# Branch units and merge of a hybrid streaming encoder: where loads and stores are issued, and how deep they are buffered

## The chip, the cores and the metric

The kernel runs on 1 core of one Trainium2 chip. The metric is device time in microseconds (us) of one execution, as the median of several runs.

## The reference, cut to what matters

One step of a one-layer encoder: 1024 frames of a new stream (the prompt) and 64 frames of a running one (the sample), 1088 frames in all, with 1024 channels. The part around the change is the mixer:

```python
def mixer(xn, conv_prefix, attn_fn, w_in, w_conv, w_conv_out, w_attn_out, w_out):
    proj = xn @ w_in
    cb, cc, ch, q, k, v, ga, gb = jnp.split(proj, splits, axis=-1)
    cv, conv_state = causal_conv(cc * ch, conv_prefix, w_conv)
    ya = (cb * cv) @ w_conv_out
    o, new_k, new_v = attn_fn(heads(q), heads(k), heads(v))
    yb = o.reshape(B, L, ATT_DIM) @ w_attn_out
    merged = jax.nn.sigmoid(ga) * ya + jax.nn.sigmoid(gb) * yb
    return merged @ w_out, conv_state, new_k, new_v
```

Ahead of it stands an RMSNorm, behind it the residual, a SwiGLU FFN with its own norm and residual, and a last norm. Everything is fp32. The kernel gets fp32 accuracy from fp32r matmuls by splitting each operand into a high part (a cast on ScalarE, line 128) and a low part (a subtraction on VectorE, line 129): three matmuls, high x high, high x low and low x high, make one product.

## The kernel before, in words

The frames are the moving side, in two halves of 544 columns (HT): 512 prompt frames and 32 sample frames each. A half is two pieces of 272 (HN).

**Units.** A `Unit` (line 202) is a block of a weight matrix, 256 output channels wide. `run` (line 253) multiplies it in seven steps (`STEPS`, line 134) instead of eight block products, after Strassen's manner; the sums of weight blocks are made by `Unit.prep` on DVE. A unit has `nk` row tiles per block: four in the units of `w_in`, where a step is 24 matmuls, and two in the four ya units, where it is 12. After a step ScalarE copies the bank to a staging place (`shot`, line 259), or VectorE adds a copy to the bank (`done`). Steps 1, 6, 5 and 3 write one bank, tagged A; steps 7 and 4 another, D. While a unit runs, `ahead` prepares the weights of the next one. Each unit's raw weights come by one load on SP into `rpool` (line 82), which has two buffers of 8 KB a partition under one tag, `raw`.

The list `units` (line 530) runs q, k, cc, ch, ga, cb, cc, ch, ga, cb, ga and then ya0 to ya3. The ya units multiply `w_conv_out` with the gated convolution, whose operand forms are made in the SBUF scratch `scr` during unit 12 (`uforms`, line 674). `ya_done` (line 697) multiplies a result with its gate row (`gated_load`, line 691, brings it back from `ga_d`) and stores it by SP to `y_d`; ya3 is stored without the gate, whose rows come later as `ga_rows`. Results and snapshots sit in four places of `scr` (`SNAP`, line 365), taken in turn by `slot` (line 369): a ya unit takes four.

**Plan.** The weights of the gates and of `w_attn_out` are listed in `plan` (line 300): ten entries of 128 channels for the gates gb 0 to 7 and ga 6 and 7, then eight for the attention output. Two entries share one load (a pair), also in `rpool`. `prep` (line 309) loads and splits them; `next_w` (line 325) calls it two entries ahead. `plain_load(0)` is called at the start of the last unit, n = 16, and `PlainNext` (line 803) prepares three entries during it.

**Gates and attention.** Gate rows gb are multiplied in four pieces each (`gate`, line 877) and stored by GpSimd to `gb_d`; between pieces `between` (line 1101) takes some steps of attention. `head_load` (line 902) brings the next head's rows by SP.

**Merge.** For each m of 8 output row tiles (line 1157): the attention product yb, then sigmoid(gb), times yb, plus the ya row, split into `mg` and, for the sample frames, `ms`. `rows_in` (line 1109) loads a row `yg` of `y_d` and a row `gb` of `gb_d`, each 128 x 1088, into the tiles that the queries had: `yg` in tag q1 with three buffers, `gb` in tag q0 with two. Two rows are asked for ahead of the loop, and row m + 2 at the end of step m.

**Output product.** `wo_half(0)` (line 1192) loads half of `w_out` and splits it into eight moving pairs; the loop at line 1249 multiplies nine tiles of frames in `ORDER` (line 171: 8, 0, 1, 4, 2, 5, 3, 6, 7). Tile 8 is the 64 sample frames, read from `ms`; the others are read from `mg`. The results go by GpSimd to `x1_d`, and a second loop, over the other half of `w_out`, reads them back.

The order of instructions in an engine's queue is not that of the code: the framework orders each queue by its own estimate of when things become ready, and puts in the waits. Within a queue the order is then fixed.

Of the kernel before, what the change touches and what calls it, by code (L numbers as in the profile page):

```python
# [8 lines left out]
F32 = mybir.dt.float32  # L9
# [6 lines left out]
P = 128  # L16
# [4 lines left out]
T = TP + TS  # L21
# [11 lines left out]
HT = T // 2  # L33
# [33 lines left out]
def encoder_kernel(ctx: ExitStack, tc: tile.TileContext, ins, outs):  # L67
    nc = tc.nc
# [131 lines left out]
        return temps[1][:, temps[0] % 2]  # L200

    class Unit:
        def __init__(self, src, nm, nk=4):
            self.nm, self.nk = nm, nk
            self.raw = rpool.tile([P, 2 * nk, 2 * P], F32, tag="raw", name=f"raw{nm}")
            nc.sync.dma_start(self.raw, src.rearrange("(k p) n -> p k n", p=P))
            self.w, self.s1 = {}, None

        def block(self, r, c):
            nk = self.nk  # L210
# [89 lines left out]
    plan = []  # L300

    def plain_load(i):
        ld, kt, at = plan[i]
        if "raw" not in ld:
            raw = rpool.tile([P, kt, ld["w"]], F32, tag="raw", name=f"rawp{i}")
            nc.sync.dma_start(raw, ld["src"].rearrange("(k p) n -> p k n", p=P))
            ld["raw"] = raw

    def prep(upto):
        while prep.n < min(upto, len(plan)):  # L310
            plain_load(prep.n)
            ld, kt, at = plan[prep.n]
            w = []
            for k in range(0, kt, 4):
                nm = f"p{prep.n}_{k}"
                hi, lo = pair(nm, ld.get("at", 0))
                split(hi, lo, ld["raw"][:, k : k + 4, at : at + P])
                w.append((hi, lo))
            plan[prep.n] = w
            prep.n += 1  # L320
# [43 lines left out]
    V32 = [10288]  # L364
    SNAP, STAGE, CC, UT = [544 * i for i in range(4)], [2720, 3808, 9264], [4896, 5988], [7080, 8172]
    KF = [CC[0], 2176, CC[1]]
    turn = {}

    def slot(places, n):

        k = turn[tuple(places)] = turn.get(tuple(places), -1) + 1
        a = places[k % len(places)]
        return scr[:, a : a + n]
# [157 lines left out]
    for nm, u in (  # L531
# [2 lines left out]
    ):  # L534
        base = {"q": C_Q, "k": C_K, "cc": C_CC, "ch": C_CH, "cb": C_CB, "ga": C_GA}[nm]
        units.append((nm, u, w_in[:, base + 2 * u * P : base + 2 * (u + 1) * P]))
    for u in range(4):
        units.append(("ya", u, ins["w_conv_out"][0][:, 2 * u * P : 2 * (u + 1) * P]))

    def unit_of(n):  # L540
        nm, u, src = units[n]
        return Unit(src, f"{nm}{u}", 2 if nm == "ya" else 4)

    normed(ORDER[0])
    normed(ORDER[1])
# [27 lines left out]
    late, due = [], []  # L573

    def snap1(key, nm):
        return slot(SNAP, HT)

    def whole(t, src, snap):

# [3 lines left out]
        else:  # L583
            vec.tensor_tensor(two, src, snap, op=ALU.add)

    def summed(src, snap):

        if snap is None:
            t = snap1(None, None)
            whole(t, src, None)  # L590
            return t
        vec.tensor_tensor(snap, src, snap, op=ALU.add)
        return snap.rearrange("p j n -> p (j n)")
# [55 lines left out]
    def row_of(dst, u, r, h):  # L649
        return dst[(2 * u + r) * P : (2 * u + r + 1) * P, h * HT : (h + 1) * HT]  # L650
# [40 lines left out]
    def gated_load(u):  # L691
        at = [CC[0], CC[0] + HT, CC[1], CC[1] + HT] if u % 2 == 0 else [STAGE[j] + i * HT for j in range(2) for i in range(2)]
        for a, (r, h) in zip(at, ((0, 0), (1, 1), (1, 0), (0, 1))):
            t = gated[u, r, h] = scr[:, a : a + HT]
            nc.sync.dma_start(t, row_of(ga_d, u, r, h))

    def ya_done(u):
        def f(r, h, src, snap):
            if u == 3:
                s = summed(src, snap)  # L700
            else:
                g = gated.pop((u, r, h))
                if snap is None:
                    s = snap1(None, None)
                    two = [t.rearrange("p (j n) -> p j n", j=2) for t in (s, g)]
                    vec.tensor_tensor(two[0], src, two[1], op=ALU.mult)
                else:
                    s = summed(src, snap)
                    vec.tensor_tensor(s, s, g, op=ALU.mult)
            nc.sync.dma_start(row_of(y_d, u, r, h), s)  # L710

        return f

# [109 lines left out]
    for n in range(len(units)):  # L823
        if n in (5, 6):
            for j in range(2):
                table_store(2 * (n - 5) + j)
        if n in (4, 5):
            for j in range(2):
                table_load(2 * (n - 4) + j, slot(STAGE, 768))
        if n == 0:  # L830
            r, si = r0, 2
        else:
            if n + 1 < len(units):
                nxt_unit = unit_of(n + 1)
                new = [(nxt_unit, {1: (), 2: (0, 1, 2)} if n == 1 else {})]
            else:
                new = [(PlainNext(), {})]
                plain_load(0)
            if n == 1:
                ahead += new  # L840
                r, si = r1, 2
            else:
                r, si = run1(n, unit, new), 0
            unit = nxt_unit
        if n >= 12 and n < 15:
            gated_load(n - 12)
        for _ in r:
            if n == 12:
                uforms(si)
            if n < 2 and si in (2 + n, 5 + n):  # L850
                i = 2 * n + si // 5
                cache_tile(i)
                if i + 2 < 4:
                    cache_load(i + 2)
            if si > 1:
                for f in due:
                    f()
                due.clear()
            due += late
            late.clear()  # L860
            si += 1
# [195 lines left out]
    def row_tile(l, nm):  # L1057
        return qp.tile([P, T], F32, tag=f"q{l}", name=nm, bufs=2 + l)
# [48 lines left out]
    rows = {}  # L1107

    def rows_in(m):
        t, z = rows[m] = row_tile(1, f"yg{m}"), row_tile(0, f"gb{m}")  # L1110
        nc.sync.dma_start(z, gb_d[m * P : (m + 1) * P])
        nc.sync.dma_start(t, y_d[m * P : (m + 1) * P])

# [13 lines left out]
    for i in range(4, len(GATES)):  # L1127
        gate_w[i] = next_w()
        if i == len(GATES) - LAST:
            for _ in steps:  # L1130
                pass
            att_stack.close()
            uo = pg_stack.enter_context(tc.tile_pool(name="uo", bufs=1, reuse_waits="tile"))
            uo.tile([P, 48], F32, name="pad_ob")
            t = uo.tile([P, 2, 4 * T + 8], F32R, name="ob")[:, :, : 4 * T]
            ob = Acts(t.rearrange("p l (k t) -> p l k t", k=4))
            ga_rows = [uo.tile([P, T], F32, name=f"ga{m}") for m in (6, 7)]
            for k in range(2):
                split(ob.t[:, 0, k], ob.t[:, 1, k], o_rows[k])
            late_r = row_tile(1, "rc2"), row_tile(0, "rc3")  # L1140
            for k, r in zip((2, 3), late_r):
                o = ob.t[:, 0, k].bitcast(F32)
                nc.sync.dma_start(o, o_d[k * P : (k + 1) * P])
                rc_load(r, k)
                vec.tensor_tensor(r, o, r, op=ALU.mult)
                split(ob.t[:, 0, k], ob.t[:, 1, k], r)
            rows_in(0)
            rows_in(1)
        for c in range(4):
            gate(i, (c,))  # L1150
            between()
# [4 lines left out]
    psum2 = pg_stack.enter_context(tc.tile_pool(name="psum2", bufs=2, space=PSUM, reuse_waits="tile"))  # L1156
    for m in range(8):
        wb = next_w()
        t, z = rows.pop(m)
        act.activation(z, z, AF.Sigmoid)  # L1160
        if m >= 6:
            vec.tensor_tensor(t, t, ga_rows[m - 6], op=ALU.mult)
        for h in range(2):
            yb = psum2.tile([P, 2, 512], F32, tag="mm", name=f"yb{m}_{h}")
            for j in range(2):
                product(yb[:, j, :HN], wb, ob, h * HT + j * HN, HN)
            hs = slice(h * HT, (h + 1) * HT)
            zh, th = z[:, hs], t[:, hs]
            two = zh.rearrange("p (j n) -> p j n", j=2)
            vec.tensor_tensor(two, yb[:, :, :HN], two, op=ALU.mult)  # L1170
            vec.tensor_tensor(th, th, zh, op=ALU.add)
            split(mg.at(0, m, h * HT, HT), mg.at(1, m, h * HT, HT), th)
            split(ms[:, m, 0, 32 * h : 32 * h + 32], ms[:, m, 1, 32 * h : 32 * h + 32], th[:, 512:])
        if m + 2 < 8:
            rows_in(m + 2)
    pg_stack.close()


# [62 lines left out]
    if True:  # L1241
# [4 lines left out]
        two_sums = early.tile([P, 2, D], F32, tag="raw", name="two_sums")  # L1246
        taken[0] += 1
        w = wo_half(0)
        for i in ORDER:
            t0, n = TT[i]  # L1250
            xt = wp.tile([P, D], F32, tag="xg", name=f"xr{i}")[:, :512]
            nc.sync.dma_start(xt[:n], x_rows(i)[:, :512])
            ps = bank2("BD", f"wo0_{i}")[:, 0]
            token_product(ps, i, mg_rows(i), KD, lambda k: w[k])
            residual(i, ps, xt, 512, f"o0_{i}")
            nc.gpsimd.dma_start(x1_d[t0 : t0 + n, :512], xt[:n])
# [563 lines left out]
```

## Time and profile before

| | us |
|---|---|
| median of 3 runs | 1474.4 |
| lowest, highest | 1472.62, 1477.31 |
| the profiled execution | 1474.73 |
| its span, first to last instruction | 1472.9 |
| TensorE busy in the span | 1451.7 |
| VectorE busy | 1002.8 |
| ScalarE busy | 688.0 |
| GpSimd busy | 131.8 |

The profile is of one execution. "PE Aya L274 <- ACT scr L261" reads: the TensorE instruction of line 274 that writes a tile Aya waited for the ScalarE instruction of line 261 that writes `scr`. In a row of the timeline the idle time ahead of an instruction and what ended it stand in brackets. A matmul's record is longer than its share of the pipeline: matmuls that follow each other overlap, so the time of a group is taken from start to start. Some names: `rawya` is the raw weight of a ya unit, `rawp` that of a pair of the plan, `wor` that of `w_out`. SPq is SP's queue of transfers, POOLq GpSimd's.

### The profile page before, as it was taken

The numbers are of one execution on the slowest core, as the hardware profiler recorded it, in microseconds if no ns is written. First come the engines' busy times: TensorE is split into PE (matmuls) and PEld (weight loads), VectorE is DVE, ScalarE is ACT, GpSimd is POOL, SyncE is SP. The second block draws the span as 40 slices with busy tenths as digits, with TensorE's granted clock in tenths as the row PEclk, the third lists the DMA queues.
The fourth block names the chain that finished last, engine by engine and source line by source line (L and its number), as shares of the span: only waits on it lengthen the run. The fifth ranks groups of instructions, "written<-read, shape, count | busy, mean of one in ns | idle before, by whom it ended". The sixth has DMA issues, their size and how long they took to land.

```text
span 1472.9 us, 26291 instructions
## 1 busy us (share of the span) xinstructions
PE 1451.7 (99%) x10128; PEld 1362.4 (92%) x10128; DVE 1002.8 (68%) x1845; ACT 688.0 (47%) x1368; POOL 131.8 (9%) x241
## 2 busy tenths in 40 slices
PE   9999999999999999999999999999999999999997
PEld 6899999999999998997889999999999999888886
DVE  7975565658347778583489767666666668957676
ACT  7654443435356777541356444444444445512223
POOL 1400010000011111000000111110111111000000
PEclk9999999999999999999999999999999999999999
DMA  8686521225876666664432443443344448867675
GB/s 287 183 272 224 193 66 64 66 86 167 261 211 187 183 187 193 211 201 130 149 119 80 153 164 143 168 140 119 130 158 164 151 160 304 288 233 249 213 267 205
DMA packets 161597, 262.49 MB, mean 178 GB/s; under 512 B 18528, under 2 KB 94496, under 8 KB 161472
## 3 DMA queue, kind: packets, MB, share of 16 engines
q1 hardware_dynamic: 140928, 196.13, 42.0%
q0 software_dynamic: 19392, 62.58, 11.8%
q10 hardware_dynamic: 1152, 2.10, 0.4%
q8 instruction: 80, 1.31, 0.4%
q14 instruction: 45, 0.37, 0.1%
HBM read 171.78 MB, written 90.81 MB: 178 GB/s over the span
## 4 chain that ended last, share of the span: by engine, by line
PE 88%; DVE 5%; DMA 3%; ACT 2%; issue 1%; SPq 0%; DVEq 0%; ACTq 0%
PE Ab L274 9%; PE Aa L274 8%; PE A L1733 8%; PE Db L274 4%; PE Da L274 4%; PE D L1733 4%; PE g L339 2%; PE g L340 2%; PE Aga L274 2%; PE g L338 2%; PE B L1733 2%; PE Ba L274 2%; PE Bb L274 2%; PE wo L1214 2%; PE wo L1216 2%; PE wo L1215 2%
## 5 line engine op out<-in xcount | busy, mean ns | idle before, releaser
L338 PE MATMUL g<-xn,wp 128*128 128x272 f32 x320 | 94.0, 294 | 0.0
L339 PE MATMUL g<-xn,wp 128*128 128x272 f32 x320 | 93.4, 292 | 0.0
L340 PE MATMUL g<-xn,low 128*128 128x272 f32 x320 | 93.3, 291 | 0.0
L128 ACT CAST ring<-w2r 128x512 fp32r<-128x512 f32 (+1 forms) x78 | 43.1, 588 | 97.1 <-PE A L1733 50.9
L937 DVE CUSTOM_DVE_ANT_0 p<-s,bb 128x640 f32<-128x640 f32 (+5 forms) x72 | 47.5, 661 | 39.8 <-PE s L980 37.5
L1733 PE MATMUL A<-ring,low 128*128 128x512 f32 x264 | 72.4, 389 | 0.0
L1733 PE MATMUL A<-ring,ht 128*128 128x512 f32 x264 | 72.2, 389 | 0.0
L129 DVE TENSOR_TENSOR low<-rawa,wa 128x512 fp32r<-128x512 f32 x55 | 37.8, 688 | 42.0 <-ACT wa L128 42.0
L338 PEld LDWEIGHTS g<-xn,wp 128*128 128x128 f32 x320 | 60.3, 188 | 0.9
L339 PEld LDWEIGHTS g<-xn,wp 128*128 128x128 f32 x320 | 60.2, 188 | 0.6
L340 PEld LDWEIGHTS g<-xn,low 128*128 128x128 f32 x320 | 60.3, 188 | 0.4
L1733 PEld LDWEIGHTS A<-ring,low 128*128 128x128 f32 x264 | 49.6, 188 | 10.3
L1733 PEld LDWEIGHTS A<-ring,ht 128*128 128x128 f32 x264 | 49.5, 188 | 10.3
L274 PE MATMUL Ab<-tt,wb 128*128 128x272 f32 x352 | 57.8, 286 | 0.4 <-ACT wb L128 0.4
L129 DVE TENSOR_TENSOR ring<-w2r,ring 128x512 fp32r<-128x512 f32 (+1 forms) x78 | 49.0, 648 | 13.4 <-ACT ring L128 13.4
L274 PE MATMUL Ab<-mg,wb 128*128 128x272 f32 x352 | 58.0, 286 | 0.0
L947 ACT ACTIVATE p<-p,mx 128x640 f32<-128x640 f32 (+5 forms) x72 | 50.8, 706 | 15.4 <-DVE mx L937 13.8
L274 PE MATMUL Aa<-mg,wa 128*128 128x272 f32 x352 | 57.7, 285 | 0.0
L274 PE MATMUL Aa<-tt,wa 128*128 128x272 f32 x352 | 57.7, 285 | 0.0
L128 ACT CAST wa<-rawa 128x512 fp32r<-128x512 f32 x55 | 34.0, 621 | 47.4 <-PE Ab L274 33.3
L128 ACT CAST wb<-rawb 128x512 fp32r<-128x512 f32 x55 | 34.0, 620 | 38.6 <-PE Aa L274 24.4
L1214 PE MATMUL wo<-low,mg 128*128 128x512 f32 x128 | 51.5, 402 | 0.0
(580 smaller groups left out, 4503.9 us busy)
## 6 DMA issues: line engine op xcount, KB each, us to landing
h_d<-hq POOLq DMA_DIRECT2D x44, 512.0 KB, 4.7
ht<-h_d SPq DMA_DIRECT2D x77, 256.0 KB, 3.6
low<-h_d SPq DMA_DIRECT2D x77, 256.0 KB, 3.8
h_d<-hq_early POOLq DMA_DIRECT2D x29, 512.0 KB, 4.8
rawa<-in_w_ff SPq DMA_DIRECT2D x11, 1024.0 KB, 6.5
rawb<-in_w_ff SPq DMA_DIRECT2D x11, 1024.0 KB, 5.3
w2r<-in_w_ff SPq DMA_DIRECT2D x11, 1024.0 KB, 8.1
qd<-q_d SPq DMA_DIRECT2D x32, 272.0 KB, 4.0
```

The source lines that it names most:

```text
L128: a = act.copy(hi, src)
L129: b = vec.tensor_tensor(lo, src, hi.bitcast(F32), op=ALU.subtract)
L274: newest[0] = mm(t[:, j, :HN], w[:, k, :], x[p][:, k, l, j * HN : (j + 1) * HN], start=p in (1, 2, 7) and k == 0 and n == 0, stop=k == las ...
L338: mm(out, a, first, start=k == 0, stop=False)
L339: mm(out, a, then, start=False, stop=False)
L340: mm(out, b, p, start=False, stop=k == kt - 1)
L937: vec.tensor_tensor_reduce(out=s if len(ps.shape) == 2 else s.rearrange("p (a b) -> p a b", a=2), in0=ps, in1=bias if len(ps.shape) == 2 e ...
L947: act.activation(s, s, AF.Exp, bias=mx, scale=-1.0, accum_out=sm)
L1214: mm(ps, x(k, 0), wh, start=f, stop=False)
L1215: mm(ps, x(k, 1), wh, start=False, stop=False)
L1216: mm(ps, x(k, 0), wl, start=False, stop=e)
L1733: mm(t, ht[k][:, j, x], w[:, l], start=p in (1, 2, 7) and k == 0 and n == 0, stop=k == len(ks) - 1 and n == 2, skip_group_check=p in (6, 5 ...
```

## The change

The raw weights of the four ya units come in two loads of 512 columns, both issued when unit 13 is built, at the start of unit 12, and each unit gets a view of them. Snapshots and results of the ya units take turns in ten places: the four of before, two in the third place of `STAGE`, and four in `UT`. Their stores to `y_d` are issued by GpSimd instead of SP. `prep` asks for the load two entries on whenever it comes to an entry, and `plain_load(0)` is called at unit 14 instead of unit 16. The rows `yg` get a pool of their own with five buffers, the rows `gb` take the tags q1 and q0 by turns; three rows are asked for ahead of the merge, and row m + 3 at the start of step m. The first output loop takes the tiles 0, 1, 2, 3, 8, 4, 5, 6, 7.

```diff
@@ -200,11 +200,14 @@
         return temps[1][:, temps[0] % 2]
 
     class Unit:
-        def __init__(self, src, nm, nk=4):
+        def __init__(self, src, nm, nk=4, raw=None):
             self.nm, self.nk = nm, nk
+            self.w, self.s1 = {}, None
+            if raw is not None:
+                self.raw = raw
+                return
             self.raw = rpool.tile([P, 2 * nk, 2 * P], F32, tag="raw", name=f"raw{nm}")
             nc.sync.dma_start(self.raw, src.rearrange("(k p) n -> p k n", p=P))
-            self.w, self.s1 = {}, None
 
         def block(self, r, c):
             nk = self.nk
@@ -309,6 +312,8 @@
     def prep(upto):
         while prep.n < min(upto, len(plan)):
             plain_load(prep.n)
+            if prep.n + 2 < len(plan):
+                plain_load(prep.n + 2)
             ld, kt, at = plan[prep.n]
             w = []
             for k in range(0, kt, 4):
@@ -364,6 +369,7 @@
     V32 = [10288]
     SNAP, STAGE, CC, UT = [544 * i for i in range(4)], [2720, 3808, 9264], [4896, 5988], [7080, 8172]
     KF = [CC[0], 2176, CC[1]]
+    MORE = SNAP + [a + j * HT for a in (STAGE[2], *UT) for j in range(2)]
     turn = {}
 
     def slot(places, n):
@@ -534,12 +540,19 @@
     ):
         base = {"q": C_Q, "k": C_K, "cc": C_CC, "ch": C_CH, "cb": C_CB, "ga": C_GA}[nm]
         units.append((nm, u, w_in[:, base + 2 * u * P : base + 2 * (u + 1) * P]))
-    for u in range(4):
-        units.append(("ya", u, ins["w_conv_out"][0][:, 2 * u * P : 2 * (u + 1) * P]))
+    units += [("ya", u, None) for u in range(4)]
+    yraw = []
 
     def unit_of(n):
         nm, u, src = units[n]
-        return Unit(src, f"{nm}{u}", 2 if nm == "ya" else 4)
+        if nm != "ya":
+            return Unit(src, f"{nm}{u}")
+        if not u:
+            for e in range(2):
+                yraw.append(rpool.tile([P, 4, 4 * P], F32, tag="raw", name=f"rawya{e}"))
+                w = ins["w_conv_out"][0][:, 4 * e * P : 4 * (e + 1) * P]
+                nc.sync.dma_start(yraw[e], w.rearrange("(k p) n -> p k n", p=P))
+        return Unit(None, f"ya{u}", 2, yraw[u // 2][:, :, u % 2 * 2 * P : (u % 2 + 1) * 2 * P])
 
     normed(ORDER[0])
     normed(ORDER[1])
@@ -573,7 +586,7 @@
     late, due = [], []
 
     def snap1(key, nm):
-        return slot(SNAP, HT)
+        return slot(MORE if "ya" in nm else SNAP, HT)
 
     def whole(t, src, snap):
 
@@ -583,10 +596,10 @@
         else:
             vec.tensor_tensor(two, src, snap, op=ALU.add)
 
-    def summed(src, snap):
+    def summed(src, snap, nm=""):
 
         if snap is None:
-            t = snap1(None, None)
+            t = snap1(None, nm)
             whole(t, src, None)
             return t
         vec.tensor_tensor(snap, src, snap, op=ALU.add)
@@ -697,17 +710,17 @@
     def ya_done(u):
         def f(r, h, src, snap):
             if u == 3:
-                s = summed(src, snap)
+                s = summed(src, snap, "ya")
             else:
                 g = gated.pop((u, r, h))
                 if snap is None:
-                    s = snap1(None, None)
+                    s = snap1(None, "ya")
                     two = [t.rearrange("p (j n) -> p j n", j=2) for t in (s, g)]
                     vec.tensor_tensor(two[0], src, two[1], op=ALU.mult)
                 else:
                     s = summed(src, snap)
                     vec.tensor_tensor(s, s, g, op=ALU.mult)
-            nc.sync.dma_start(row_of(y_d, u, r, h), s)
+            nc.gpsimd.dma_start(row_of(y_d, u, r, h), s)
 
         return f
 
@@ -835,7 +848,6 @@
                 new = [(nxt_unit, {1: (), 2: (0, 1, 2)} if n == 1 else {})]
             else:
                 new = [(PlainNext(), {})]
-                plain_load(0)
             if n == 1:
                 ahead += new
                 r, si = r1, 2
@@ -844,6 +856,8 @@
             unit = nxt_unit
         if n >= 12 and n < 15:
             gated_load(n - 12)
+        if n == 14:
+            plain_load(0)
         for _ in r:
             if n == 12:
                 uforms(si)
@@ -1107,7 +1121,7 @@
     rows = {}
 
     def rows_in(m):
-        t, z = rows[m] = row_tile(1, f"yg{m}"), row_tile(0, f"gb{m}")
+        t, z = rows[m] = u_rows.tile([P, T], F32, tag="yg", name=f"yg{m}"), row_tile((m + 1) % 2, f"gb{m}")
         nc.sync.dma_start(z, gb_d[m * P : (m + 1) * P])
         nc.sync.dma_start(t, y_d[m * P : (m + 1) * P])
 
@@ -1134,6 +1148,7 @@
             uo.tile([P, 48], F32, name="pad_ob")
             t = uo.tile([P, 2, 4 * T + 8], F32R, name="ob")[:, :, : 4 * T]
             ob = Acts(t.rearrange("p l (k t) -> p l k t", k=4))
+            u_rows = pg_stack.enter_context(tc.tile_pool(name="u_rows", bufs=5, reuse_waits="tile"))
             ga_rows = [uo.tile([P, T], F32, name=f"ga{m}") for m in (6, 7)]
             for k in range(2):
                 split(ob.t[:, 0, k], ob.t[:, 1, k], o_rows[k])
@@ -1144,8 +1159,8 @@
                 rc_load(r, k)
                 vec.tensor_tensor(r, o, r, op=ALU.mult)
                 split(ob.t[:, 0, k], ob.t[:, 1, k], r)
-            rows_in(0)
-            rows_in(1)
+            for m in range(3):
+                rows_in(m)
         for c in range(4):
             gate(i, (c,))
             between()
@@ -1156,6 +1171,8 @@
     psum2 = pg_stack.enter_context(tc.tile_pool(name="psum2", bufs=2, space=PSUM, reuse_waits="tile"))
     for m in range(8):
         wb = next_w()
+        if m + 3 < 8:
+            rows_in(m + 3)
         t, z = rows.pop(m)
         act.activation(z, z, AF.Sigmoid)
         if m >= 6:
@@ -1171,8 +1188,6 @@
             vec.tensor_tensor(th, th, zh, op=ALU.add)
             split(mg.at(0, m, h * HT, HT), mg.at(1, m, h * HT, HT), th)
             split(ms[:, m, 0, 32 * h : 32 * h + 32], ms[:, m, 1, 32 * h : 32 * h + 32], th[:, 512:])
-        if m + 2 < 8:
-            rows_in(m + 2)
     pg_stack.close()
 
 
@@ -1246,7 +1261,7 @@
         two_sums = early.tile([P, 2, D], F32, tag="raw", name="two_sums")
         taken[0] += 1
         w = wo_half(0)
-        for i in ORDER:
+        for i in (0, 1, 2, 3, 8, 4, 5, 6, 7):
             t0, n = TT[i]
             xt = wp.tile([P, D], F32, tag="xg", name=f"xr{i}")[:, :512]
             nc.sync.dma_start(xt[:n], x_rows(i)[:, :512])
```

## The prediction

> **What bounds the kernel now.** I read the page first: who is busy, and for what share of the span.
>
> ```profile
> PE 1451.7 (99%) x10128; PEld 1362.4 (92%) x10128; DVE 1002.8 (68%) x1845; ACT 688.0 (47%) x1368; POOL 131.8 (9%) x241
> ```
>
> TensorE is the bound, and 1472.9 - 1451.7 = 21.2 us is all that it ever stands idle. An edit that removes no matmul can win only there, and in matmuls that run at less than their usual pace. So the second view is the table of waits of TensorE alone (us in total, times, longest).
>
> ```profile
> PE Aya L274 <- ACT scr L261: 3.1, 2, 1.9
> PE wo L1218 <- DVE ms L129: 1.7, 1, 1.7
> PE t L1026 <- ACT pt L128: 1.4, 1, 1.4
> PE Aya L274 <- DVE scr L592: 1.3, 1, 1.3
> PE yb L338 <- DVE gb L1170: 0.9, 1, 0.9
> ```
>
> These six waits make 8.4 us and all lie where the diff is: the ya units, the split of plan weights during attention, the merge with yb, and the start of wo. The rest is the start, short waits, and the tail after the last matmul; no edit reaches those. The third view, stages cut into windows, says that the FFN has nothing to give. Its columns are the window, its length, and busy us (instructions) of PE, PEld, DVE, ACT and POOL, then granted clock, DMA share and GB/s.
>
> ```profile
> 342.00:353.00 11.00, 11.00 (x91) 11.00 (x91) 10.10 (x22) 6.03 (x14) 0.00 (x0) 1.00 0.61 202
> 342.00:390.00 48.00, 43.58 (x347) 42.93 (x347) 34.78 (x68) 20.89 (x44) 0.63 (x5) 1.00 0.68 215
> 604.00:668.00 64.00, 63.13 (x505) 62.91 (x504) 45.42 (x74) 27.63 (x53) 0.00 (x0) 1.00 0.68 219
> 800.00:900.00 100.00, 100.00 (x813) 100.00 (x812) 70.38 (x119) 45.75 (x87) 11.18 (x21) 1.00 0.41 144
> ```
>
> The fourth view, the chain that ended last, names what stands behind the waits: transfers.
>
> ```profile
> 352.35 2.96 PE Aya L274 x24
> 366.55 6.12 DMA y_d<-scr
> 378.55 6.30 DMA y_d<-scr
> 561.50 6.40 DMA rawp<-in_w_attn_out
> 654.97 7.73 DMA yg<-y_d
> 1254.23 5.44 PE A L1733 x24
> ```
>
> **Part 1: the ya units (two loads, ten places, GpSimd's queue).** Start of the first ya matmul, the three stalls, and the first gate matmul behind the stage, from the timeline of TensorE:
>
> ```profile
> 343.31 0.66 PE L274 MATMUL Aya<-xs,wya 128*128 128x272 f32 x4
> 364.01 0.77 PE L274 MATMUL Aya<-xn,wya 128*128 128x272 f32 x4 [1.30 <-DVE scr L592]
> 373.42 0.77 PE L274 MATMUL Aya<-xs,wya 128*128 128x272 f32 x4 [1.23 <-ACT scr L261]
> 385.60 0.76 PE L274 MATMUL Aya<-xs,wya 128*128 128x272 f32 x4 [1.88 <-ACT scr L261]
> 390.16 0.29 PE L338 MATMUL g<-xn,wp 128*128 128x272 f32 x1
> ```
>
> The stage takes 390.16 - 343.31 = 46.85 us. Undisturbed, 24 matmuls take 2.96 us, so 4 units x 84 matmuls need 14 x 2.96 = 41.44 us: 5.4 us are lost. A step of 12 matmuls is 1.48 us, and the step after next accumulates into the bank that ACT or DVE must copy first, so a copy late by more than about a step stops TensorE. What made the copies late:
>
> ```profile
> 362.90 0.42 DVE L225 TENSOR_TENSOR sf<-rawya 128x256 f32<-128x256 f32 x1 [2.44 <-DMA rawya<-in_w_conv_out]
> 372.75 0.61 ACT L261 COPY scr<-Aya 128x544 f32<-128x544 f32 x1 [2.21 <-DMA y_d<-scr]
> 384.21 0.62 ACT L128 CAST wp<-rawp 128x512 fp32r<-128x512 f32 x1 [1.51 <-DMA rawp<-in_w_in]
> ```
>
> The first is a weight load issued while the unit before runs. After the change both halves are asked for a unit before ya0 starts, in buffers that the units cb1 and ga2 have left, so each has a unit of 168 matmuls, 7 x 2.96 = 20.7 us, or more to land. The second is a staging place whose store has not landed. With four places a place comes round after one unit, 10.4 us; with ten after 2.5 units, 26 us, which covers the 6.1 and 6.3 us of the chain with much to spare. The third is the plan's weights; their first load moves from the last unit to two units earlier, once ya1 has left its buffer, and the second pair is asked for with the first. I count the whole 5.4 us.
>
> What it costs: the bytes stay the same (two loads of 1 MB for four of 0.5 MB), the views into them are free, and 16 stores leave SP for GpSimd's queue. Price and landing on each side:
>
> ```profile
> 394.16 0.55 POOL L888 DMA_DIRECT2D gb_d<-gst  x1 [4.42 <-ACT gst L887]
> y_d<-scr SPq DMA_DIRECT2D x16, 272.0 KB, 4.1
> gb_d<-gst POOLq DMA_DIRECT2D x32, 136.0 KB, 3.5
> SPq L710 <- DVE scr L709: 19.9, 8, 5.9
> ```
>
> 16 x 0.55 = 9 us of issuing on an engine busy for 0.63 of these 48 us; behind the waiting stores stand only its memsets for attention and the gates' stores. The landing may be as quick as 3.5 us or as slow as the chain's 6.3 us; 26 us hide both, so I take zero, and if the cover were gone a stall would be of the old size, 1.2 to 1.9 us each. On SP the 19.9 us in which it stood at these stores no longer hold up the loads behind.
>
> **Part 2: plan weights a pair ahead.** In attention one cast waited for such a load (that of 561.50), and TensorE for the cast's engine:
>
> ```profile
> 567.92 1.14 ACT L128 CAST wp<-rawp 128x512 fp32r<-128x512 f32 x2 [1.38 <-DMA rawp<-in_w_attn_out]
> 568.79 0.29 PE L338 MATMUL g<-xn,wp 128*128 128x272 f32 x1
> 570.46 0.74 PE L1026 MATMUL t<-ident,p 128*128 128x128 f32 x5 [1.38 <-ACT pt L128]
> ```
>
> The gap from 568.79 to 570.46 against the usual 0.12 us (2.96/24) is 1.5 us; loaded a pair earlier, it goes. The price is on SP: each such load now waits for the last split of the pair whose buffer it takes, with the next head's loads queued behind it. The nearest row, below among the rivals, has 2.7 us as its longest wait; a gate's four pieces of 24 matmuls are 11.8 us at the pace above, so I take zero and keep 2.7 each as the bound.
>
> **Part 3: output rows.** DVE stood for yg from 654.97 to 662.73, and then TensorE:
>
> ```profile
> 664.28 0.29 PE L340 MATMUL yb<-ob,low 128*128 128x272 f32 x1
> 665.44 0.39 PE L338 MATMUL yb<-ob,wp 128*128 128x272 f32 x1 [0.87 <-DVE gb L1170]
> ```
>
> 1.16 us where 0.12 is usual, and about 0.1 on the next: 1.1 us. Three rows ahead, each 6 us of matmuls, are 18 us against 7.73. The loads' number is unchanged.
>
> **Part 4: new frames fifth.** The first wo tile reads ms, which is written last. The tiles 0 to 3 read only the first half of mg. The fourth row is a window on TensorE: busy us, granted clock, DMA share, GB/s.
>
> ```profile
> 671.63 0.50 PE L1219 MATMUL wo<-wo,ms 128*128 128x512 f32 x1
> 673.81 0.50 PE L1218 MATMUL wo<-low,ms 128*128 128x512 f32 x1 [1.67 <-DVE ms L129]
> 678.25 0.40 PE L1215 MATMUL wo<-low,mg 128*128 128x512 f32 x1
> 674.00:678.00 4.00, 4.00 (x12) 0.60 0.99 308
> 672.13 0.68 DVE L129 TENSOR_TENSOR wo<-wor,low 128x512 fp32r<-128x512 f32 x1
> ```
>
> From 671.63 to 678.25 thirteen matmuls start, 6.62 us; a 512-column matmul takes 5.44/24 = 0.23 us, thirteen 3.0: 3.6 us lost, 1.67 waiting and 2.0 at a granted clock of 0.60 right behind the wait. What is late next is the last low weight half, done at 672.8. The matmul at 671.63 is the fourteenth of wo, so the first starts at about 668.6. Tile 0, in its place, needs that half for its 24th matmul, 23 x 0.23 = 5.3 us on, at 673.9: 1.1 us in hand, so I count zero here, and 1.1 us or so if the splits are queued later.
>
> [...] The wait here was 1.67 us, and a 1.88 us wait in ya was followed by a clock of 1.00. [...]
>
> **The sum.** 5.4 + 1.5 + 1.1 + 3.6 = 11.6 us. I take off one wait of the size of those seen (the six long ones average 1.4 us), since DVE must do its 34.8 us of the ya units in 41.4, 0.84 of the time, and a new short wait is likely somewhere: 10.2. The profiled execution took 1474.73 us, so 1464.5; the median of the runs is 0.3 lower, 1464.2.
>
> **The rivals.** (a) The dip is not the wait's: 2.0 us stay, 1466.2. For it, the clean clock after 1.88 us in ya; for the wait, it is the longest loss and lies right ahead of the dip. (b) In ya another wait takes over, at that load of DVE: half of 5.4 comes back, 1466.9. Against it, in ya0 DVE was busy for 10.1 of 11 us and TensorE for all 11. (c) The edit of the code does not move the queues: loads were already issued ahead of their place in the code, as buffers came free, and land where they did; only wo's order acts, 3.6 us: 1470.8. Against it, the four places and the shared SP queue are facts of the storage, which no order mends. (d) The rows' loads, now six of 544 KB before the first yb, go ahead of the last attention rows: 3.3 MB at 219 GB/s is 15 us; if half of that shows on TensorE, 1472. Against it, they stand behind those loads in the code. (e) Slower: SP stands at the plan's loads in attention with head loads behind.
>
> ```profile
> SPq L306 <- DVE low L129: 6.9, 5, 2.7
> DVE p L937 <- DMA kd<-k_d: 0.9, 1, 0.9
> ```
>
> The second row shows the heads' lead to be nil at least once. Five pairs x 2.7 = 13.5 us of stalls make 11.6 into a loss of 1.9, and each can cost a clock dip of 2.0: 1476.3 to 1486, say 1480. It decides once SP stands longer at such a load than a head's rows are early; against it, one gate's 12 us between load and use.
>
> **How the numbers follow.** Forecast 0.56, (a) 0.12, (b) 0.12, (c) and (d) 0.06 each, (e) 0.08. Anything within 0.3%, 4.4 us, is about what a measurement of this kernel cannot tell from no change; so faster is the forecast with (a) and (b), 0.80; the same is (c) and (d), 0.12; slower is (e), 0.08. The likeliest case alone runs from 1462.8, all 11.6 us, down to 1461 with the runs' own spread, up to 1467. For 8 in 10 the range goes on through (a), (b) and (c) to 1472.
>
> **What would show it.** Right: no wait over 0.5 us in the ya units, which take about 41.5 us; no cast waiting for rawp; no yg wait; wo starting without a pause at a clock of 1.00. Wrong: ACT copies in ya waiting for y_d stores on GpSimd's queue, s or p waiting for qd or kd, yb waiting for ob, or a pause before the 24th wo matmul.

## The result and the profile after

The changed kernel takes 1471.97 us (median of 22 runs, 1469.37 to 1475.97), the kernel before 1475.5 us on the same chip (22 runs, 1471.44 to 1478.81). The ratio is 0.9979, with an interval of 0.9971 to 0.9988: 3.1 us shorter, 1.8 to 4.3. That lies within the 0.3% that the prediction calls no change. The forecast was 10.2 us.

The profiled execution of the changed kernel took 1471.99 us. Its page, the line of the engines, and then TensorE's waits (us in total, times, longest):

```profile
PE 1452.0 (99%) x10128; PEld 1363.1 (93%) x10128; DVE 1001.2 (68%) x1845; ACT 687.8 (47%) x1368; POOL 140.9 (10%) x257
```

```profile
PE t L1040 <- DVE pt L129: 4.1, 5, 3.3
PE warm L454 <- ACT ones L452: 2.9, 1, 2.9
PE xt L1302 <- DVE xg L1291: 0.6, 1, 0.6
...
PE yb L343 <- DVE gb L1187: 0.3, 1, 0.3
PE wo L1229 <- DVE xr L1247: 0.3, 1, 0.3
```

The waits of the ya units are gone, yb waits 0.3 us in place of 0.9, and wo 0.3 in place of 1.7. Line 1040 is line 1026 of before: one transposition of attention now waits 3.3 us, longer than any of the six waits of before. The windows by stage, with the columns of before:

```profile
342.00:390.00 48.00, 47.91 (x388) 47.69 (x387) 35.55 (x69) 21.89 (x46) 9.89 (x22) 1.00 0.66 218
460.00:540.00 80.00, 75.70 (x518) 69.14 (x517) 55.08 (x136) 52.98 (x127) 11.69 (x22) 0.96 0.64 170
604.00:668.00 64.00, 63.69 (x510) 63.47 (x509) 45.71 (x76) 27.73 (x53) 0.00 (x0) 1.00 0.59 207
668.00:690.00 22.00, 21.70 (x99) 17.64 (x98) 6.30 (x12) 3.73 (x7) 1.68 (x3) 1.00 0.54 185
```

and the second of them in the kernel before:

```profile
460.00:540.00 80.00, 79.56 (x564) 72.89 (x565) 58.12 (x146) 56.55 (x139) 14.11 (x27) 1.00 0.67 186
```

In the ya units TensorE is busy 47.91 of 48 us where it was 43.58, and wo starts at a clock of 1.00. But between 460 and 540, in the middle of attention, it is busy for 3.9 us less, and the granted clock is 0.96. The chain of work that ended last in the stretch from 486 to 502 tells why:

```profile
488.27 0.58 SPq L944
488.86 0.05 issue
488.91 0.02 SPq L309
488.92 0.03 issue
488.95 8.38 DMA rawp<-in_w_in
497.33 0.02 issue
497.36 0.63 ACT wp L128
497.99 0.02 issue
498.01 0.69 DVE low L129
498.70 0.75 DVE pt L129
499.45 0.04 issue
499.49 1.33 PE t L1040 x5
```

SP issues the load of plan entries 8 and 9 behind the loads of a head. It lands 8.38 us later, then ScalarE casts, VectorE subtracts and only then makes the low part `pt` that the transposition needs. The same place in the timeline:

```profile
488.95 0.53 SPq L309 DMA_DIRECT2D rawp<-in_w_in  x1
495.88 0.29 PE L343 MATMUL g<-xn,wp 128*128 128x272 f32 x1
497.36 0.62 ACT L128 CAST wp<-rawp 128x512 fp32r<-128x512 f32 x1 [4.42 <-DMA rawp<-in_w_in]
498.01 0.69 DVE L129 TENSOR_TENSOR low<-rawp,wp 128x512 fp32r<-128x512 f32 x1 [3.63 <-ACT wp L128]
499.49 1.33 PE L1040 MATMUL t<-ident,p 128*128 128x128 f32 x5 [3.33 <-DVE pt L129]
503.40 0.43 PE L345 MATMUL g<-xn,low 128*128 128x272 f32 x1
505.83 0.29 PE L343 MATMUL g<-xn,wp 128*128 128x272 f32 x1
```

ScalarE came to the cast at 497.36 - 4.42 = 492.94, 4.0 us after the load was issued, and stood there; what attention wanted of it stood behind the cast. No gate needs this weight yet: entry 8's gate is the ninth and starts at 590.38, and at the cast's turn the fifth is just ending. After TensorE's pause a matmul of 272 columns lasts 0.43 us in place of 0.29 until about 505.7. TensorE in windows of 4 us (busy, clock, DMA share, GB/s):

```profile
496.00:500.00 4.00, 0.67 (x5) 0.84 0.63 165
500.00:504.00 4.00, 4.00 (x16) 0.50 0.11 39
504.00:508.00 4.00, 4.00 (x29) 0.81 0.35 94
```

So the one wait costs 3.3 us of idleness and about half of the 6 us from 499.5 to 505.6: some 6.3 us. In stages (us; ya from the first ya matmul to the first gate matmul, attention from there to the first yb matmul of line 339, 344 in the changed kernel, merge to the first wo matmul, wo to the first FFN matmul, FFN up to the first matmul that writes `ys`):

| profiled execution of | ya | attention | merge | wo | FFN up |
|---|---|---|---|---|---|
| before | 46.85 | 229.43 | 48.97 | 105.48 | 464.62 |
| after | 41.82 | 235.43 | 48.41 | 102.33 | 464.62 |

5.0 + 0.6 + 3.1 = 8.7 us are won and 6.0 lost: 2.7, and the spans differ by 1472.9 - 1470.1 = 2.8. Each row is one execution. Two profiles of the same instructions differ by up to 1.4 us in a stage (wo_alone below, ahead of wo), so the 0.6 us of the merge are not shown to come from the edit.

### The profile page after: what moved, and what is told of

Read it like the earlier page. It is cut to its first block, busy times and chain, and to the rows that moved or that the text cites. A ratio compares the mean times of both kernels' runs of the same rounds, so it can differ in the third digit from the quotient of the medians.

```text
span 1470.1 us, 26272 instructions
## 1 busy us (share of the span) xinstructions
PE 1452.0 (99%) x10128; PEld 1363.1 (93%) x10128; DVE 1001.2 (68%) x1845; ACT 687.8 (47%) x1368; POOL 140.9 (10%) x257
## 4 chain that ended last, share of the span: by engine, by line
PE 76%; issue 12%; DVE 6%; DMA 3%; ACT 2%; POOL 0%; SPq 0%; ACTq 0%; POOLq 0%; DVEq 0%
PE Ab L277 9%; PE Aa L277 8%; PE A L1748 8%; PE Db L277 4%; PE Da L277 4%; PE D L1748 4%; PE g L344 2%; PE g L345 2%; PE g L343 2%; PE B L1748 2%; PE Ba L277 2%; PE Bb L277 2%; PE wo L1229 2%; PE t L1040 2%; PE wo L1231 2%
```

## The experiments

The theories: **A**, the loads a pair ahead make SP issue a load where its cast stops attention; **B**, the other edits do, by moving queues. Both say that the cast stands too close behind its load. The first four kernels ran on one chip beside the kernel before (median 1474.83 us there); held_on_before, held_no_ahead, held_four_places and wo_alone on one beside it (1474.56); held_one, held_yd_on_sp and held_old_rows on one beside it (1474.46).

**ahead_ya_only**, the first of those four. The changed kernel with the load a pair ahead only for the entries that are split in the ya units:

```diff
-            if prep.n + 2 < len(plan):
+            if prep.n < 4:
                 plain_load(prep.n + 2)
```

> The changed kernel, but the pair ahead is asked for only by the first four entries of the plan (those split during the ya units); in attention each pair is loaded as before the change. Theory A (the pair-ahead edit in attention made the new wait of 3.3 us and the clock dip behind it): the stretch from the first gate matmul to the first full yb product, 229.4 us before and 235.3 us after the change, falls to 229 to 230, and the time to about 1466.5 us, 0.6% under the kernel before. Rival B (any shift of what stands ahead of attention makes the queues fall out differently, and the wait comes from the ya edits): the stretch stays at 234 to 236 and the time at 1472.

1469.46 us, ratio 0.9964 (0.995 to 0.9979). In the profile its attention stage took 237.5 us, and the wait is still there, at another load, with the scores of a head behind it:

```profile
447.44 0.53 SPq L309 DMA_DIRECT2D rawp<-in_w_in  x1
456.36 1.14 ACT L128 CAST wp<-rawp 128x512 fp32r<-128x512 f32 x2 [4.23 <-DMA rawp<-in_w_in]
459.16 0.58 PE L993 MATMUL s<-kd,qd 128*128 128x256 f32 x1 [4.26 <-DVE mx L951]
```

So the loads a pair ahead in attention are not needed for the stall: without them the cast is due 4.7 us behind its load, and the stall is as large. But the profiled execution took 1474.3 us, the longest of the seven and 4.8 us over their median, and the median lies between what A and B expected. How often the stall comes in this kernel is not shown.

**ahead_att_only.** The kernel before with the load a pair ahead from entry 4 on, and nothing else:

```diff
             plain_load(prep.n)
+            if 4 <= prep.n < len(plan) - 2:
+                plain_load(prep.n + 2)
```

> The kernel before, with the pair ahead asked for by the entries from the fifth on, that is in attention and behind; nothing else of the change. Theory A: the stretch from the first gate matmul to the first full yb product grows from 229.4 to about 235 us and a cast waits over 3 us for rawp; the time is about 1480 us, 0.3% over the kernel before. Rival B: the stretch stays at 229 to 230, or loses the 1.5 us wait at 569 us, and the time is 1474 to 1475.5.

1477.08 us, ratio 1.0014 (1.0005 to 1.0024): a loss of 2.1 us (0.7 to 3.5), attention 230.4 us in the profile. Alone, the loads a pair ahead bring nothing and cost a little. A expected a cast waiting over 3 us and 1480 us; the longest such wait is 1.1 us.

**ya_alone.** The kernel before with part 1 but for the plan: two loads for the ya weights, ten places, stores on GpSimd's queue.

> The kernel before with the ya edits alone: two raw loads, ten places, stores to y_d by GpSimd. Theory A: the ya units take 41.5 to 44 us instead of 46.85 (the first plan weights still come late), attention keeps its 229.4 us, the time is about 1471 us, 0.3% under the kernel before. Rival B: the ya units gain the same, but a new wait of a cast for rawp in attention gives 4 to 6 us back, and the time is about 1475.

1472.69 us, ratio 0.9988 (0.9973 to 1.0003), runs from 1468.2 to 1480.6. The ya stage is 41.5 us, but 5.4 us less there show as about 2 in the median. Edits that end before attention have moved attention's loads and casts: the plan's fourth load is issued at 445.35 us, at 473.25 in the kernel before, and its cast waits 1.36 us. Attention took 230.7 us in the profile, with a wait of TensorE of 1.4 us. These 1.2 us over the kernel before are no more than two profiles of the same instructions differ, and the profiled execution, 1468.2 us, is the shortest of the twelve: its span is 6.5 us under that of the kernel before. So B rests on ahead_ya_only; where the longer executions of ya_alone lose their gain, no trace shows.

**held_splits.** The changed kernel; each split from attention on is queued behind the newest copy of a gate piece, so that no cast runs ahead of its place in the code:

```diff
+    behind = [None]
...
-                split(hi, lo, ld["raw"][:, k : k + 4, at : at + P])
+                if behind[0] is None:
+                    split(hi, lo, ld["raw"][:, k : k + 4, at : at + P])
+                else:
+                    with tc.issue_after(behind[0]):
+                        split(hi, lo, ld["raw"][:, k : k + 4, at : at + P])
...
-            act.copy(st[:, :n], ps[:, :n])
+            behind[0] = act.copy(st[:, :n], ps[:, :n]).ins
```

> The changed kernel, with each cast of a plan weight from attention on queued behind the copy of the last gate piece ahead of it in the code, so that it stands on ScalarE's queue later than the queue's own order would put it; loads are not held. Theory A2 (the wait arises since the cast stands close behind its load's issue, long before its weights are needed): no cast waits for rawp in attention, the stretch from the first gate matmul to the first full yb product falls from 235.3 to 228 to 230 us and the time to 1465 to 1467, under both kernels. Rival C (the load's traffic itself, 1 MB among the heads' rows, costs the time, wherever the cast stands): the stretch stays at 234 to 236, with waits for qd, kd or bb instead, and the time at about 1472.

1466.38 us (1464.65 to 1467.63), ratio 0.9943 (0.993 to 0.9956). Attention 229.4 us, no wait of TensorE over 0.6 us but the first.

**held_one.** Which cast is it? The changed kernel with that hold for entry 8 alone (`if prep.n != 8: split(...)`, else held); the loads stay where they were.

> The changed kernel with one edit: the split of plan entry 8 alone stands in its queues behind the newest gate copy (entry 9, of the same load, follows it); entries 0 to 7, all loads and their places on SP stay as they are. If the cast of entry 8, queued close behind its load, is what cost the changed kernel its gain, attention falls from 235.4 us to 229.4 and the time from 1472.0 to about 1466.5, as in held_splits. If several splits share the loss, or the loss is in the loads, the attention stage stays at 232 us or more and the time at 1469 or more.

1465.5 us, ratio 0.9947 (0.9933 to 0.9961). The load and its first cast, TensorE's longest waits behind the first, and the window of attention:

```profile
488.89 0.53 SPq L309 DMA_DIRECT2D rawp<-in_w_in  x1
553.73 1.14 ACT L128 CAST wp<-rawp 128x512 fp32r<-128x512 f32 x2
```

```profile
PE warm L459 <- ACT ones L457: 2.9, 1, 2.9
PE pvv L528 <- ACT low L128: 0.8, 1, 0.8
PE xt L1307 <- DVE xg L1296: 0.6, 1, 0.6
```

```profile
460.00:540.00 80.00, 79.25 (x567) 73.05 (x567) 58.19 (x143) 56.31 (x133) 12.23 (x23) 1.00 0.67 184
```

The load is issued at the same microsecond as in the changed kernel (488.95), the cast now 65 us behind it, and attention takes 228.3 us in place of 235.4. So the load by itself cost nothing; the place of its casts (the two of entry 8, with those of entry 9 behind them) was the whole loss. Up to 495 us TensorE, VectorE and ScalarE have the same instructions in the same order in both kernels. Behind that the framework has ordered others anew as well, and what this does by itself was not tried.

**held_on_before.** The same hold as held_splits, on the kernel before.

> The kernel before with nothing but the hold: each split of plan weights from attention on stands in its queue behind the newest gate copy. The plan's loads keep their places on SP. If casts that are queued close behind their loads are what stops attention, the wait of 1.4 us near 568 goes, no wait of TensorE of over 1 us is left in attention, the runs scatter less, and the time is 1 to 2 us lower than the kernel before. If attention has another limit, the stage stays at 229.4 us and the time is the same within 0.5 us. If the hold only helps where the change has moved the loads, holding costs something here: casts come late for their gates, yes with waits of TensorE for wp.

1474.4 us, ratio 1.0003 (0.9992 to 1.0015), runs from 1472.45 to 1479.35. The wait of 1.4 us is gone, yet the stage took 229.1 us. Up to the last head the gain is there (the first transposition `rt` of the eighth head starts 203.7 us behind the first gate matmul, 204.9 in the kernel before) and it is given back after that, where all splits for `w_attn_out` now stand behind the last copy of a gate piece. The stretch from 590 to 620, held and then before:

```profile
590.00:620.00 30.00, 29.41 (x229) 28.52 (x228) 17.93 (x27) 19.36 (x36) 2.56 (x5) 1.00 0.77 232
```

```profile
590.00:620.00 30.00, 30.00 (x234) 29.09 (x233) 15.64 (x24) 16.09 (x30) 2.56 (x5) 1.00 0.64 193
```

In the kernel before, the hold gains nothing; it mends what the change broke. That the runs would scatter less was wrong.

**held_no_ahead.** held_splits without the loads a pair ahead in attention (the edit of ahead_ya_only).

> held_splits, with the load a pair ahead limited to the four entries that are split in the ya units; in attention a pair's load is asked for as in the kernel before. If the place of the split in its queue is what counts, the load a pair ahead is worth nothing once splits are held: the same time as held_splits within 1 us, attention at about 229.4 us. If the load a pair ahead carries the gain, casts wait for rawp again, attention is 2 us or more longer, and the time is 1468.5 or more.

1465.03 us (1464.97 to 1466.75), ratio 0.9937 (0.9924 to 0.9949). Once the splits are held, the loads a pair ahead in attention are worth nothing that shows.

**held_four_places.** held_splits with `MORE = SNAP`.

> held_splits, with the ya units back in four staging places; the two loads and the stores on GpSimd's queue stay. If staging places whose stores have not landed were what stalled the ya units, copies wait for y_d stores again: waits of Aya or Dya for scr of 1 to 2 us each, the ya stage at 43.5 to 46 us in place of 41.5, and the whole 2 to 4.5 us longer than held_splits. If stores standing in SP's queue were the cause, GpSimd's queue mends it alone: the stage stays at 41.5 us and the time is that of held_splits.

1471.94 us, ratio 0.9985 (0.9973 to 0.9997), 5.6 us longer than held_splits. In the profile, whose execution was the longest of the ten (1476.83 us), the ya stage took 50.1 us. ScalarE's copies wait for stores to `y_d` to land, the matmuls for the copies, and the granted clock was 0.93 from 346 to 398:

```profile
366.26 0.61 ACT L264 COPY scr<-Aya 128x544 f32<-128x544 f32 x1 [4.34 <-DMA y_d<-scr]
366.92 1.27 PE L277 MATMUL Aya<-xs,wya 128*128 128x272 f32 x4 [3.74 <-ACT scr L264]
391.37 0.61 ACT L264 COPY scr<-Aya 128x544 f32<-128x544 f32 x1 [2.00 <-DMA y_d<-scr]
392.04 0.77 PE L277 MATMUL Aya<-xs,wya 128*128 128x272 f32 x4 [1.66 <-ACT scr L264]
```

**held_yd_on_sp.** held_splits with the stores to `y_d` on SP again.

> held_splits with the stores to y_d on SP's queue again; ten places and two loads stay. If the ten places are what frees the ya units, the stage stays at 41.5 us and the time within 1 us of held_splits: GpSimd's queue is worth nothing by itself. If stores waiting on SP for their results hold up the loads behind them, the plan's loads or the first head's rows come later: a wait for wp at the first gates or for a cast behind rawp, and 1 to 3 us more.

1467.15 us, ratio 0.9947 (0.9932 to 0.9961), ya stage 41.4 us. The ten places are what counts; GpSimd's queue makes no difference that these runs can tell. In its profile yb waited once, 3.3 us, for a row (merge 52.9 us); the interval shows nothing of it, and why it came was not tried.

**held_old_rows.** held_splits with the rows of the merge as before.

> held_splits with the rows of the merge as in the kernel before: two rows ahead, three buffers for yg, row m + 2 asked for at the end of step m. By part 3 of the prediction, yb waits for gb again by 0.8 us or so, the merge takes 49.0 us in place of 48.6, and the time is 1 us longer than held_splits. The rival: the merges of kernels with the old rows have already been seen at 47.9 to 49.3 us, so the rows make nothing that shows: the time is that of held_splits within 1 us, with no wait of TensorE in the merge.

1466.15 us, ratio 0.9946 (0.9934 to 0.9958). yb waits 1.2 us for `gb`, the merge takes 49.4 us: the wait returns as expected, and the time does not show it. Whether rows bring 1 us or nothing is below what these runs tell.

**wo_alone.** The kernel before with the order of the output tiles alone.

> The kernel before with the order of the first output loop alone changed (tiles 0, 1, 2, 3, 8, 4, 5, 6, 7). If part 4 of the prediction holds, the wait for ms of 1.67 us goes and the reduced clock behind it with it: the wo stage falls from 105.4 us to 102.4, and the whole by 3 us. If the dip has a source of its own (rival a), the stage falls by about 1.4 us alone, to about 104, and some 4 us at a granted clock of 0.6 stay near the start of wo. If the order moves the wait to another tile, the stage stays at 105.

1472.02 us, ratio 0.998 (0.9971 to 0.9989): 2.9 us shorter, 1.6 to 4.3. The wo stage took 101.8 us, without a pause, at a clock of 1.00 from 668 to 690. Ahead of wo TensorE, VectorE, ScalarE and GpSimd have the same instructions in the same order as in the kernel before, and yet this profile shows 48.21 us for ya (with a wait of 2.6 us), 230.61 for attention and 47.83 for the merge: 1.1 to 1.4 us more or less, with nothing edited there.

## Why the prediction was wrong

**The step that failed** stands in part 2: "a gate's four pieces of 24 matmuls are 11.8 us at the pace above, so I take zero and keep 2.7 each as the bound". It measures from the load to the gate that uses the weight. But the cast stands in ScalarE's queue, the subtraction in VectorE's, and while the cast waited for its load, both engines stood idle (4.42 and 3.63 us): what counts is the time from the load to the cast's turn. Entry 8's gate was 101 us behind its load (488.95 to 590.38), its cast's turn 4.0. The framework orders each queue by its own estimate, so a cast can stand far ahead of its use; the prediction used this only in rival (c), as a reason that edits might not act. They moved queues that they did not touch. When the cast's turn comes (its start less the wait in brackets), against the load's issue:

| kernel | load issued | cast's turn | later by | wait |
|---|---|---|---|---|
| before | 539.89 | 547.20 | 7.3 | 0.22 |
| ya_alone | 445.35 | 451.68 | 6.3 | 1.36 |
| ahead_att_only | 495.19 | 500.26 | 5.1 | 1.12 |
| ahead_ya_only | 447.44 | 452.13 | 4.7 | 4.23 |
| after | 488.95 | 492.94 | 4.0 | 4.42 |
| held_one | 488.89 | 553.73 | 64.8 | none |

The row of before was in the trace, ahead of the cast of 567.92 that the prediction quotes (its turn came 5.0 us behind the load of 561.50, and it waited 1.38):

```profile
547.42 0.62 ACT L128 CAST wp<-rawp 128x512 fp32r<-128x512 f32 x1 [0.22 <-DMA rawp<-in_w_in]
```

A cast with no slack, where the plan's loads took from 4.3 to 9.1 us to land, median 6.2, was the warning: by these numbers a turn 4 us earlier would have stopped ScalarE and VectorE for some 4 us. Why the framework put the cast just there was not tried.

**Sizes.** In attention the sum had 1.5 gained less 1.4 for one new wait, 0.1 in all; it became a loss of 6.0. The allowance for a wait was made, from the mean of six, but without the clock behind it: the wait came to 3.3 us idle and some 3.0 at half clock. That step is 6.1 of the 7.4 us between 10.2 and the profiles' 2.8; the rest are the small shortfalls below, each within what two profiles of the same instructions differ.

**Part 1** was right: 5.0 of 5.4 us, and held_four_places shows that without the staging places the gain goes. That the copies wait for stores, the prediction read from brackets; the runs show also that the change of queue, which it priced at zero, is worth nothing that shows. The earlier call of `plain_load(0)`, which it held to end the third stall, moved nothing: ya_alone does without it, its first plan load is issued at 353.95 us, 353.66 in the changed kernel, and no matmul of its ya units waits. What the two large loads bring by themselves was not tried. **Part 3** came to 0.6 of 1.1 us in the stage, which shows nothing: kernels with the old rows took 47.8 to 49.4 us for the merge, those with the new ones 47.8 to 48.6 (52.9 in held_yd_on_sp). **Part 4** was right in its place: 3.1 of 3.6 us, 2.9 by itself. Tile 0 did not wait: its last low half was done at 672.11 and its 24th matmul started at 674.00, 1.9 us later, where the prediction held 1.1 to be in hand. The one wait there, 0.3 us at 680.19, is the third tile's, for the bank of the first.

**The rivals.** (e) named part 2 as the danger, but by SP: SP standing at plan loads and heads' rows late. SP's longest stand at such a load, 18.6 us, lies in the ya units, in the changed kernel and in held_one alike; in attention it is 0.4 us in the changed kernel, 2.9 in held_one, and no matmul of either waits for `qd` or `kd`. (b) and (d) did not come: no matmul of the ya units waits, and none of the merge waits for `ob`. (c) held for the call of `plain_load(0)` alone. (a) is open to both sides. Before had the wait of 1.67 us and the dip behind it; ya_alone and held_on_before have the same wait, 1.67 and 1.68 us, with wo stages of 103.9 us. TensorE in windows of 4 us, ya_alone and then held_on_before:

```profile
668.00:672.00 4.00, 3.24 (x14) 1.00 0.73 250
672.00:676.00 4.00, 4.00 (x20) 1.00 0.57 152
```

```profile
668.00:672.00 4.00, 3.49 (x15) 1.00 0.02 5
672.00:676.00 4.00, 2.84 (x12) 1.00 0.59 206
676.00:680.00 4.00, 4.00 (x19) 1.00 0.67 189
```

Before and ahead_att_only (the latter 0.95 and 0.63 behind its 1.67 us) dip. So the dip follows the wait in some kernels and not in others, and in three where wo starts without the wait (after, held_one, wo_alone) the clock from 668 to 690 is 1.00; the dip's 1.6 us (105.5 - 103.9) are not sure to be won. Behind longer waits the dip came each time here: leaving out the first 50 us, the thirteen profiles have five waits of TensorE of over 2 us (2.6, 3.3, 3.3, 3.7 and 4.3). In the changed kernel the clock was 0.50 from 499.5 to 505.6, behind its 3.33 us, with matmuls of 272 columns of 0.43 us where 0.29 is usual; each of the other four profiles has such matmuls of 0.43 us too, in the stage of its wait. In the eight without so long a wait no matmul that writes `Aya`, `g` or `yb` lasted over 0.40 us, though they have waits of up to 1.9 us there. In the kernel before, four of the five waits of 1.1 to 2.0 us (1.23, 1.30, 1.38 and 1.88) were followed by 4 us at a clock of 1.00; only that at wo had a dip. Why 1.67 us is followed by a dip in two kernels of four was not shown.

With its splits held in place, the change brings most of the 10.2 us that were forecast: 7.8 us (5.8 to 9.9) in held_one, 9.3 (7.5 to 11.2) in held_no_ahead.

## What to carry to other kernels

For a load whose consumer stands in an engine's queue, measure from the load's issue to the consumer's turn in that queue, not to the last use of the data; a cast that already waits 0.2 us behind its load has no slack, and an edit a stage away can use it up. After an edit, read the waits of stages that it did not touch, and pin a split that was hoisted far ahead of its need to a point close to it. Price a long wait of TensorE with the half clock behind it: here every wait of 2.6 us or more, behind the first 50 us of a profile, was followed by matmuls of 0.43 us in place of 0.29, and 3.3 us of waiting cost 6.3.

## What the runs showed that was not expected

The same wait, 1.67 us at the start of wo, was followed by a granted clock of 0.60 to 0.63 in two kernels and by 1.00 in two others. Instructions that an edit left in the same order took up to 1.4 us more or less in a stage from one profile to the next. A load of 1 MB behind a head's loads landed after 8.38 us in the changed kernel; the five such loads of the plan in the kernel before took 6.0 to 7.7 us.
